# A hybrid attention and recurrent layer: the order of the first loads, and who copies x^T

## The chip, the cores and the metric

The kernel runs on one core of a Trainium2 chip. The metric is device time in microseconds (us) of one execution, the median of several. The engines of a core are TensorE (PE; its weight loads are shown apart as PEld), VectorE (DVE), ScalarE (ACT), GpSimd (POOL) and SyncE (SP, which only issues DMAs here). Each engine runs its own instructions in the order in which they stand, and waits on semaphores for the others.

## The reference

One inference step of a single decoder layer, for 1024 prompt tokens and 8 x 4 sample tokens (1056 together) with a paged cache of 1024 rows for each of the 8 sample sequences. Cut to what matters here:

```
u = rmsnorm(x, norm_mix)                       # 1056 x 1024
z = u @ w_in                                   # q, six k/v parts, gates, two RG-LRU branches
kc, vc = compress(kv rows and cached pages)    # blocks of 32 rows, stride 16, two small matmuls
o = gates * (attend(q, kc, vc), selected blocks, window of 512)
h = rglru(rx)                                  # conv of width 4, gates, a scan over time
x = x + [rmsnorm(o), rmsnorm(gelu(rg) * h)] @ w_out
x = x + square(relu(rmsnorm(x) @ w_up)) @ w_down
y = rmsnorm(x)
```

All of it is in float32. The kernel keeps that accuracy by writing each factor of a matmul as a sum of a high and a low part and taking three products.

## The kernel before

The kernel is written in stages. A list scheduler then sets each engine's order from its own estimate of times: an instruction goes where the estimate says that it can start, and `high_priority` moves a block of code ahead by a number of places. So the order on an engine is not the order of the code, and a change in one place moves rows elsewhere.

The stage that the change touches is the first, `run` up to `cmp_cached`:

- `fetch_x` loads nine tiles of x, eight of 128 tokens x 1024 (512 KB each) and one of 32 sample tokens, by SP. The pool gives eight buffers to the tag `xt`, so the ninth load waits until the first tile has been used.
- `pages_setup` loads the page table twice: to one partition for SP's registers, and as 64 single numbers to two partitions (`pt2`, issued by ACT), from which DVE casts `pf`, PE makes `ps_pg` and DVE the row numbers `idx` for POOL's gathers.
- `load_x` works in three groups of three tiles (the last has 288 columns, the others 384). ACT squares each tile with a running sum into `ss` (`xj`). Then, for each of eight blocks `kb` of 128 features, PE transposes the group's tiles into one PSUM bank, `ps_x` (even blocks from a pool of three buffers, `tp`, odd ones from a pool of two, `mm`). Three instructions empty the bank: ACT writes the scaled high part `u_hi`, DVE the rest `u_lo`, and a plain copy `xr` goes out to DRAM as x^T (`xT_dram`, POOL issues the store, one for two blocks). Of the eight `xr` copies of a group ACT makes two, DVE six.
- `w_tile` loads one 512 KB tile of w_in into the single buffer `wraw` (SP) and splits it: `wh` on ACT, `wl` on DVE. It runs at high priority, so the first of these loads stands ahead of x.
- `cmp_setup` loads the two compression weights (`cwraw`, one buffer) and splits them: the high part on ACT, the low part on POOL. `vectors` loads nine small vectors as rows of one tile (`rows`, nine DMAs of POOL), has PE turn it (`ps_vec`) and derives constants for the RG-LRU on DVE (`sp_w`, `sp_s`, `sp_acc`, `cneg`, `cpos`: a chain of tiny instructions).
- `norm_x` makes 1/rms of all tokens (`ms`, `rxi`, `rxt`, `rxy`), puts them on diagonals (`dg`, DVE), and PE spreads them over the partitions (`ps_bc`, nine products of which one is small); ACT copies the result to `R`. The first products of the layer, `ps_in` (two tiles of z, 144 matmuls), are scaled by `R` as they leave PSUM.
- `cmp_cached` gathers pages of the cache (`lpg`: half by SP, half by indirect DMAs of POOL, three buffers), copies them apart (`lpr`, POOL and DVE), and PE transposes them (`ps_ct`) for the compression matmuls `ps_c`.

DMAs of SP and ACT signal eight semaphores in turn, and a later one with the same semaphore is issued only once the earlier one has landed. After this stage come the RG-LRU, the attention (from about 400 us on) and the MLP (from about 790 us to the end).

## Time and profile before

| | |
|---|---|
| median of 3 runs | 1569.31 us (1569.22 to 1573.13) |
| profiled execution | 1570.45 us; its span 1568.7 us |
| PE busy | 1475.2 us, 94% of the span |
| PEld, DVE, ACT, POOL busy | 88%, 57%, 39%, 28% |
| mean granted TensorE clock | 0.969 |
| first matmul, first `ps_in` | 6.88 us, 42.30 us |

PE is busy almost throughout, so the time is that of PE's work and of the places at which PE has none. The largest such place is the start of the program. In the page's 40 slices of 39.2 us the first has PE at five tenths, and the DMA engines there are busy at nine tenths and move 296 GB/s, the most of all slices.

### The profile page before, as it was taken

The page shows a single profiled execution, that of the slowest core. Times are in us where ns is not written, and L with a number is a line of the kernel's source. Part 1 is how long each engine was busy: PE and PEld are TensorE (multiplying, and loading weights), DVE is VectorE, ACT ScalarE, POOL GpSimd, SP SyncE. Part 2 cuts the span into 40 slices and gives each one's busy share as a digit, 9 for nine tenths or more (in the row PEclk, how much of TensorE's full clock was granted, in tenths as well). Part 3 has the DMA queues.
Part 4 walks back from the last instruction along what each step waited for, and adds up shares of the span by engine and source line. Part 5 has one row for each costly group of instructions (what it writes and reads, how often), then busy time and mean ns, then how long its engine had stood idle before and what let it go on. Part 6 is the DMA issues. An engine that isn't in the chain of part 4 may idle for free.

```text
span 1568.7 us, 24573 instructions
## 1 busy us (share of the span) xinstructions
PE 1475.2 (94%) x9445; PEld 1381.3 (88%) x9445; DVE 890.5 (57%) x1671; ACT 615.0 (39%) x1216; POOL 440.2 (28%) x533
## 2 busy tenths in 40 slices
PE   5989999999899779999899999999999999999997
PEld 3979999999776547777898999999999999999997
DVE  6664788556687638988687343333424343342445
ACT  6253775122487528777354031220303122030322
POOL 6540143342585318767473000000000000000012
PEclk9999999999799959999999999999999999999999
DMA  9544413352013310000512020330202021020102
GB/s 296 159 149 114 125 28 106 126 174 83 28 55 90 100 55 1 1 28 28 165 47 63 13 81 28 113 102 26 69 14 81 28 68 41 19 76 14 41 13 99
DMA packets 127961, 115.53 MB, mean 74 GB/s; under 512 B 16752, under 2 KB 115760, under 8 KB 127716
## 3 DMA queue, kind: packets, MB, share of 16 engines
q1 hardware_dynamic: 122446, 102.10, 21.4%
q0 software_dynamic: 3200, 8.67, 1.8%
q10 hardware_dynamic: 2198, 3.20, 0.7%
q8 instruction: 74, 1.21, 0.3%
q14 instruction: 43, 0.35, 0.1%
HBM read 98.17 MB, written 28.32 MB: 81 GB/s over the span
## 4 chain that ended last, share of the span: by engine, by line
PE 76%; DVE 10%; ACT 6%; issue 3%; DMA 3%; POOL 2%; SPq 1%; ACTq 0%; DVEq 0%; POOLq 0%
PE ps_dn L122 8%; PE ps_dn L123 8%; PE ps_dn L124 8%; PE ps_up L122 7%; PE ps_up L123 7%; PE ps_up L124 7%; PE ps_T L1092 3%; PE ps_in L122 3%; PE ps_in L124 3%; PE ps_in L123 3%; PE ps_O L1102 2%; PE ps_out L122 2%; PE ps_out L124 2%; PE ps_out L123 2%; PE ps_O L1101 2%
## 5 line engine op out<-in xcount | busy, mean ns | idle before, releaser
L122 PE MATMUL ps_dn<-hh,wdh 128*128 128x352 f32 x768 | 248.3, 324 | 0.0
L122 PE MATMUL ps_up<-v_hi,wuh 128*128 128x352 f32 x768 | 248.1, 323 | 0.0
L123 PE MATMUL ps_up<-v_lo,wuh 128*128 128x352 f32 x768 | 246.3, 321 | 0.0
L124 PE MATMUL ps_up<-v_hi,wul 128*128 128x352 f32 x768 | 246.1, 320 | 0.0
L123 PE MATMUL ps_dn<-hl,wdh 128*128 128x352 f32 x768 | 245.9, 321 | 0.0
L124 PE MATMUL ps_dn<-hh,wdl 128*128 128x352 f32 x768 | 245.6, 321 | 0.0
L1363 DVE TENSOR_TENSOR x<-x,ps_dn 128x352 f32<-128x352 f32 x192 | 99.2, 520 | 222.2 <-PE ps_dn L124 222.2
L1428 POOL TENSOR_TENSOR facc<-facc,fsq 128x352 f32<-128x352 f32 x18 | 17.0, 942 | 700.0 <-ACT fsq L1426 699.9
L127 ACT CAST wdh<-wd 128x1024 fp32r<-128x1024 f32 x32 | 33.5, 1047 | 341.2 <-PE ps_dn L123 288.7
L123 PEld LDWEIGHTS ps_up<-v_lo,wuh 128*128 128x128 f32 x768 | 144.3, 188 | 0.0
L123 PEld LDWEIGHTS ps_dn<-hl,wdh 128*128 128x128 f32 x768 | 144.2, 188 | 0.0
L122 PEld LDWEIGHTS ps_dn<-hh,wdh 128*128 128x128 f32 x768 | 144.1, 188 | 0.0
L122 PEld LDWEIGHTS ps_up<-v_hi,wuh 128*128 128x128 f32 x768 | 144.1, 188 | 0.0
L124 PEld LDWEIGHTS ps_up<-v_hi,wul 128*128 128x128 f32 x768 | 143.9, 187 | 0.0
L124 PEld LDWEIGHTS ps_dn<-hh,wdl 128*128 128x128 f32 x768 | 143.9, 188 | 0.0
L122 PE MATMUL ps_in<-u_hi,wh 128*128 128x352 f32 x432 | 142.3, 329 | 0.0
L124 PE MATMUL ps_in<-u_hi,wl 128*128 128x352 f32 x432 | 141.0, 326 | 0.0
L123 PE MATMUL ps_in<-u_lo,wh 128*128 128x352 f32 x432 | 140.6, 326 | 0.0
L128 DVE TENSOR_TENSOR ptl<-ps_T,pth 128x512 fp32r<-128x512 f32 x132 | 87.7, 684 | 14.4 <-ACT pth L127 13.2
L127 ACT CAST pth<-ps_T 128x512 fp32r<-128x512 f32 (+1 forms) x148 | 83.1, 587 | 23.3 <-PE ps_T L1092 18.0
L122 PEld LDWEIGHTS ps_in<-u_hi,wh 128*128 128x128 f32 x432 | 82.6, 191 | 0.6 <-issue 0.3
L123 PEld LDWEIGHTS ps_in<-u_lo,wh 128*128 128x128 f32 x432 | 82.8, 192 | 0.1
(511 smaller groups left out, 3232.4 us busy)
## 6 DMA issues: line engine op xcount, KB each, us to landing
wu<-in_w_up_dram SPq DMA_DIRECT2D x32, 512.0 KB
wd<-in_w_down_dram SPq DMA_DIRECT2D x32, 512.0 KB
wraw<-in_w_in_dram SPq DMA_DIRECT2D x18, 512.0 KB
slc_dram<-in_cache_kv_dram SPq DMA_DIRECT2D x64, 128.0 KB
kvs<-slc_dram SPq DMA_DIRECT2D x32, 256.0 KB
xres<-xT_dram SPq DMA_DIRECT2D x8, 528.0 KB
x_dram<-xres SPq DMA_DIRECT2D x8, 528.0 KB
x<-x_dram SPq DMA_DIRECT2D x3, 1408.0 KB
```

Source lines behind the costliest of these rows:

```text
L122: t.matmul(out, wh, xh, start=first, stop=False)
L123: t.matmul(out, wh, xl, start=False, stop=False)
L124: t.matmul(out, wl, xh, start=False, stop=last)
L127: self.nc.scalar.copy(hi, src)
L128: (eng or self.nc.vector).tensor_tensor(lo, src, hi.bitcast(F32), ALU.subtract)
L1092: T.transpose(ps[:K, h * 128 : h * 128 + 128], src(h), self.ident)
L1101: T.matmul(O, v, ph, start=first, stop=False)
L1102: T.matmul(O, v, pl, start=False, stop=last)
L1363: V.tensor_tensor(x1[:, d, sl], x1[:, d, sl], ps[:, :CH], ALU.add)
L1428: P.tensor_tensor(acc, acc, sq, ALU.add)
```

## The change

- `fetch_x` runs at twice the priority offset of the weights, and each of the nine tiles has a buffer of its own.
- In `load_x` the squares stand behind the group's transposes in the code; ACT makes every even `xr` copy (four of eight), DVE the odd ones; `xr` has four buffers where it had five.
- `vectors` is cut in two. `vector_rows` issues the nine small loads, and only after the last store of x^T has been issued; their tile moves to the pool `ccp`. The rest of `vectors` runs after the first two tiles of z have been written.

```diff
-    def vectors(self):
-        nc, a = self.nc, self.a
-        rows = self.xrp.tile([56, 128], F32, name="rows")
+    def vector_rows(self):
+        nc, a = self.nc, self.a
+        self.rows56 = rows = self.ccp.tile([56, 128], F32, name="rows")
...
-            eng.dma_start(rows[r : r + n, :], src)
+            with self.tc.issue_after(self.stores[2, 7].ins):
+                eng.dma_start(rows[r : r + n, :], src)
             r += n
+
+    def vectors(self):
+        nc = self.nc
         ps = self.ps_c.tile([128, 512], F32, tag="c", name="ps_vec")
-        nc.tensor.transpose(ps[:, :56], rows, self.ident[:56, :56])
+        nc.tensor.transpose(ps[:, :56], self.rows56, self.ident[:56, :56])
...
         for grp in range(3):
             tiles = self.xt[grp * 3 : grp * 3 + 3]
-            for t, (xt, n) in enumerate(tiles):
-                junk = self.xtp.tile([128, D], BF16, tag="xj", name="xj", bufs=1)
-                nc.scalar.activation(junk[:n], xt[:n], AF.Square, accum_out=self.ss[:n, grp * 3 + t : grp * 3 + t + 1])
...
                 if kb % 2 == 0:
-                    xr = self.xrp.tile([128, 2, 384], F32, tag="xr", name="xr", bufs=5)
-                (nc.scalar.copy if kb % 4 == 0 else nc.vector.tensor_copy)(xr[:, kb % 2, :wdt], ps[:, :wdt])
+                    xr = self.xrp.tile([128, 2, 384], F32, tag="xr", name="xr", bufs=4)
+                (nc.vector.tensor_copy if kb % 2 else nc.scalar.copy)(xr[:, kb % 2, :wdt], ps[:, :wdt])
...
+            for t, (xt, n) in enumerate(tiles):
+                junk = self.xtp.tile([128, D], BF16, tag="xj", name="xj", bufs=1)
+                nc.scalar.activation(junk[:n], xt[:n], AF.Square, accum_out=self.ss[:n, grp * 3 + t : grp * 3 + t + 1])
...
-        for t in range(9):
-            n = 128 if t < 8 else 32
-            xt = self.xtp.tile([128, D], F32, tag="xt", name="xt", bufs=8)
-            nc.sync.dma_start(xt[:n], a["x_prompt"][0, t * 128 : t * 128 + 128] if t < 8 else xs)
-            self.xt.append((xt, n))
+        with self.tc.high_priority(offset=2 * HP):
+            for t in range(9):
+                n = 128 if t < 8 else 32
+                xt = self.xtp.tile([n, D], F32, name=f"xt{t}")
+                nc.sync.dma_start(xt, a["x_prompt"][0, t * 128 : t * 128 + 128] if t < 8 else xs)
+                self.xt.append((xt, n))
...
-                    self.vectors()
+                    self.vector_rows()
...
                 zs = [self.z_tile(512 + i * 128, self.zp, "z", 2) for i in range(2)]
+                self.vectors()
                 self.cmp_cached()
```

What the scheduler makes of it stands below, place by place. Line numbers of the changed kernel are up to five higher than those of before.

**The start, on ACT.** Before, behind its three DMA issues (`wraw` is the weight tile, `xj` the squares, `xr` the copy of x^T):

```order
L127 ACT_TABLE_LOAD
L127 CAST wh<-wraw 128x1024
L249 ACTIVATE xj,ss<-xt 128x1024 x3
L261 ACTIVATE u_hi<-ps_x,g_mix 128x384 x5
L249 ACTIVATE xj,ss<-xt 128x1024
L265 COPY xr<-ps_x 128x384
```

In the changed kernel, at the same place:

```order
L271 ACT_TABLE_LOAD
L271 ACTIVATE xj,ss<-xt_113 128x1024
L271 ACTIVATE xj,ss<-xt_115 128x1024
L271 ACTIVATE xj,ss<-xt_117 128x1024
L262 ACTIVATE u_hi<-ps_x,g_mix 128x384 x3
L271 ACTIVATE xj,ss<-xt_119 128x1024
L262 ACTIVATE u_hi<-ps_x,g_mix 128x384 x2
L266 COPY xr<-ps_x 128x384
```

The first three squares stay ahead of the first `u_hi`, though the code has them behind; the weight's cast `wh` has moved from the front to behind the eleventh `u_hi`.

**Before the first ps_in, on PE.** Before (the last transposes of x, the transposes of two gathered page tiles, and the first products):

```order
L257 MATMUL ps_x<-ident,xt 128x32
L593 MATMUL ps_ct<-ident,lpr_678 128x128 x4
L257 MATMUL ps_x<-ident,xt 128x128 x2
L257 MATMUL ps_x<-ident,xt 128x32
L593 MATMUL ps_ct<-ident,lpr_714 128x128 x4
L122 MATMUL ps_in<-u_hi,wh 128x352
```

In the changed kernel:

```order
L258 MATMUL ps_x<-ident,xt_129 128x32
L1173 MATMUL ps_bc<-dg,ones 128x128 x4
L598 MATMUL ps_ct<-ident,lpr_678 128x128 x4
L258 MATMUL ps_x<-ident,xt_125 128x128
L258 MATMUL ps_x<-ident,xt_127 128x128
L258 MATMUL ps_x<-ident,xt_129 128x32
L1173 MATMUL ps_bc<-dg,ones 128x128 x2
L598 MATMUL ps_ct<-ident,lpr_714 128x128 x4
L122 MATMUL ps_in<-u_hi,wh 128x352
```

Six of the products that spread 1/rms (`ps_bc`) have moved ahead of the first `ps_in`; before, all of them stood behind it.

**The end of the stores, on POOL.** Before (`cwvl` is the low part of the second compression weight, `lpr` a copy of a gathered page tile, `xT_dram` a store of x^T):

```order
L128 TENSOR_TENSOR cwvl<-cwraw,cwvh 128x1024
L586 COPY lpr_786<-lpg 128x256
L267 DMA xT_dram<-xr 128x2x288
L586 COPY lpr_899<-lpg 128x256
L586 COPY lpr_786<-lpg 128x256
L551 DMA lpg<-in_cache_kv_dram,idx_147 128x256 x2
```

In the changed kernel:

```order
L591 COPY lpr_786<-lpg 128x256
L268 DMA xT_dram<-xr 128x2x288
L200 DMA rows<-in_norm_mlp_dram 8x128
L200 DMA rows<-in_conv_w_dram 16x128
L200 DMA rows<-in_conv_b_dram 4x128
L200 DMA rows<-in_b_ra_dram 4x128
L200 DMA rows<-in_b_ri_dram 4x128
L200 DMA rows<-in_lam_dram 4x128
L200 DMA rows<-in_g_attn_dram 4x128
L200 DMA rows<-in_g_rnn_dram 4x128
L200 DMA rows<-in_norm_final_dram 8x128
L591 COPY lpr_899<-lpg 128x256
```

The nine small loads, which stood among POOL's first instructions, now stand behind the last store of x^T and ahead of copies and gathers of pages; `cwvl` has moved up, ahead of the third store from the end.

## Rows read from the trace of the kernel before

**Rows 1.** Stretches of the span: length, busy time of each engine, granted clock, DMA.

```profile
0.00:12.98 12.98, 4.46 (x18) 3.26 (x19) 2.28 (x11) 5.78 (x8) 7.60 (x18) 1.00 0.88 306
12.98:31.20 18.22, 10.88 (x44) 7.67 (x42) 15.98 (x31) 18.09 (x37) 13.78 (x15) 1.00 1.10 319
31.20:42.30 11.10, 6.92 (x26) 4.41 (x27) 10.86 (x42) 4.21 (x11) 7.06 (x11) 1.00 0.87 237
42.30:72.70 30.40, 29.07 (x182) 28.52 (x181) 17.14 (x45) 6.26 (x12) 19.25 (x25) 1.00 0.52 156
72.70:131.40 58.70, 53.45 (x419) 48.58 (x418) 36.49 (x81) 31.98 (x78) 19.77 (x39) 0.96 0.45 130
...
390.00:640.00 250.00, 215.62 (x1486) 161.17 (x1486) 173.44 (x357) 154.45 (x390) 139.96 (x195) 0.87 0.18 51
```

**Rows 2.** What PE waited for in 0 to 60 us: total, times, longest.

```profile
PE ps_x L257 <- DVE xr L265: 6.4, 5, 1.9
...
PE ps_pg L525 <- DVE pf L523: 1.6, 1, 1.6
```

**Rows 3.** ACT's first instructions in time: start, duration, what [idle before it].

```profile
2.12 1.28 ACT L127 ACT_TABLE_LOAD   x1 [2.12 <-issue]
4.99 1.04 ACT L127 CAST wh<-wraw 128x1024 fp32r<-128x1024 f32 x1 [1.59 <-DMA wraw<-in_w_in_dram]
6.83 1.06 ACT L249 ACTIVATE xj<-xt 128x1024 bf16<-128x1024 f32 x1 [0.80 <-DMA xt<-in_x_prompt_dram]
...
10.07 1.06 ACT L249 ACTIVATE xj<-xt 128x1024 bf16<-128x1024 f32 x1 [0.58 <-DMA xt<-in_x_prompt_dram]
...
12.98 1.52 ACT L261 ACTIVATE u_hi<-ps_x,g_mix 128x384 fp32r<-128x384 f32 x3 [1.76 <-PE ps_x L257]
```

**Rows 4.** DVE in order of time, around its first u_lo.

```profile
11.68 0.17 DVE L523 CAST pf<-pt 2x32 f32<-2x32 int32 x1 [3.73 <-DMA pt<-in_page_table_dram]
...
13.60 1.14 DVE L262 SCALAR_TENSOR_TENSOR u_lo<-ps_x,g_mix,u_hi 128x384 fp32r<-128x384 f32 x2 [0.61 <-ACT u_hi L261]
```

**Rows 5.** DVE's groups in 12.98 to 42.30 us: count | busy, mean ns | idle before.

```profile
L265 DVE COPY xr<-ps_x 128x384 f32<-128x384 f32 (+1 forms) x16 | 8.1, 519 | 0.0
...
L128 DVE TENSOR_TENSOR wl<-wraw,wh 128x1024 fp32r<-128x1024 f32 x1 | 1.2, 1224 | 0.7 <-ACT wh L127 0.7
...
L229 DVE SCALAR_TENSOR_TENSOR sp_acc<-sp_acc,sp_s 128x4 f32<-128x4 f32 x4 | 0.6, 156 | 0.0
```

**Rows 6.** ACT's groups in the same stretch.

```profile
L261 ACT ACTIVATE u_hi<-ps_x,g_mix 128x384 fp32r<-128x384 f32 (+1 forms) x24 | 12.8, 587 | 7.9 <-PE ps_x L257 7.8
...
L265 ACT COPY xr<-ps_x 128x384 f32<-128x384 f32 (+1 forms) x6 | 2.8, 474 | 0.0
```

**Rows 7.** DVE and POOL in order of time, at POOL's two weight splits.

```profile
28.55 2.35 DVE L586 COPY lpr<-lpg 128x256 f32<-128x256 f32 x1
...
32.95 0.28 DVE L586 COPY lpr<-lpg 128x256 f32<-128x256 f32 x1
...
43.28 0.59 DVE L1167 TENSOR_SCALAR dg<-ident,rxy 128x128 f32<-128x128 f32 x2
...
28.37 2.37 POOL L128 TENSOR_TENSOR cwkl<-cwraw,cwkh 128x1024 fp32r<-128x1024 f32 x1
...
45.88 2.41 POOL L128 TENSOR_TENSOR cwvl<-cwraw,cwvh 128x1024 fp32r<-128x1024 f32 x1
```

**Rows 8.** POOL in order of time: one small load, and a wait.

```profile
4.14 0.56 POOL L199 DMA_DIRECT2D rows<-in_norm_mlp_dram  x1
...
65.11 1.08 POOL L586 COPY lpr<-lpg 128x256 f32<-128x256 f32 x3 [6.41 <-PE ps_ct L593]
```

**Rows 9.** PE in order of time, around the first ps_in.

```profile
41.56 1.09 PE L593 MATMUL ps_ct<-ident,lpr 128*128 128x128 f32 x4 [1.56 <-POOL lpr L586]
42.30 0.64 PE L122 MATMUL ps_in<-u_hi,wh 128*128 128x352 f32 x1
...
54.30 0.68 PE L1168 MATMUL ps_bc<-dg,ones 128*128 128x128 f32 x4 [1.33 <-DVE dg L1167]
```

## The prediction

> **What bounds the kernel now.** I read the busy shares first: PE works 94% of the span, so a change pays only where PE has nothing to do or waits. Next the stretches [rows 1]. Up to the first `ps_in` at 42.30 us, PE is busy 4.46 + 10.88 + 6.92 = 22.3 us, with transposes alone; in the 30.4 us behind it, 29.07. The change works on the first 42.3 us, and each microsecond by which `ps_in` starts earlier shifts what follows, as long as nothing later holds PE up.
>
> What sets those 42.3 us? In 12.98 to 31.20 ACT is busy 18.09 of 18.22 us; in 31.20 to 42.30 DVE is busy 10.86 of 11.10 [rows 1]. PE's longest wait behind the first load is for DVE's `xr` copies, 6.4 us in five waits [rows 2], because a PSUM bank is free only after `u_hi`, `u_lo` and `xr`. ACT in turn waited 7.8 us for PE [rows 6], late in the stage. So there are two phases: until x has landed the loads set the pace, then ACT, and DVE at the end. The last step is a wait of 1.56 us for POOL's copy of a page tile [rows 9].
>
> **x ahead of the weights.** The weight tile landed at 4.97 us and the first x tile at 6.83, the third at 10.05 (ACT was waiting for each) [rows 3]. That is 1.6 to 1.8 us a tile of 512 KB. Without a weight tile ahead of it the third x tile should land some 1.6 us earlier, at about 8.4. ACT's table load now stands behind the first tile's arrival and takes 1.28 us, which is hidden: the tile comes at about 5.1, the load ends at 6.4, two squares of 1.06 end at 8.5, the third at 9.6. ACT's first `u_hi` moves from 12.98 to about 9.7. DVE cannot follow that far. Its cast of the page list stands ahead of its first `u_lo`, and the list landed at 11.68 after 3.73 us of waiting [rows 4]. The list's load has not moved, so the first `u_lo` goes from 13.60 to 11.85: **-1.75 us** (0 if the list lands 1.75 later, -3.7 if it no longer matters). PE's own stop of 1.6 us at `ps_pg` [rows 2] has the same cause and stays, with fifteen transposes done ahead of it. The ninth buffer frees SP from a wait before its first page load; SP's other page loads follow earlier by as much, and no one waits for them here.
>
> By the Trainium skill (DMA: Bandwidth & Descriptors, Issuing engines are not separate DMA queues), transfers of all issuing engines share the same 16 DMA engines and interleave. By that the page list, on ACT's queue, gains nothing from a new order on SP's; the trace agrees so far as it shows the list landing at 11.68 us, amid DMA engines 88% busy.
>
> **Copies from DVE to ACT.** Before the first `ps_in` DVE makes 11 copies, where it made 16 at 8.1/16 = 0.51 us [rows 5]: -2.5. ACT makes 11 where it made 5, at 2.8/6 = 0.47 [rows 6]: +2.8. ACT was busy 18.09 + 4.21 = 22.3 us between 12.98 and 42.30 [rows 1]. The order puts ahead of `ps_in` also the second weight's cast and the second compression weight's (1.04 each by the cast in rows 3) and a copy of `R` (0.6, the size of a `u_hi` [rows 6]): 22.3 + 2.8 + 2.1 + 0.6 = 27.8. Begun at 9.7 that ends at 37.5. ACT has 4.8 us to spare against 42.3, so its copies cost nothing by themselves; without that cover they would cost 2.8.
>
> **DVE's own sum.** Besides -2.5 for copies: the tiny chain behind `vectors`, 14 or so instructions of 156 ns that overlap by half [rows 5], leaves: -1.2 (-2.2 by full durations). The second `wl` comes in, +1.2 [rows 5]; three pairs of `dg` at 0.5 to 0.59 [rows 7], +1.5; the rest of the rms chain, +0.5; one more `lpr` copy, +0.3. Net **-0.2 us** (-1.2 to +0.6): DVE does other work in the place of what it loses, and that work is what it had to do later.
>
> DVE idled 29.32 - 15.98 - 10.86 = 2.5 us in 12.98 to 42.30 [rows 1], mostly for ACT. ACT now starts 3.3 us earlier, DVE 1.75; half of the idle time should go: **-1.2** (0 to -2.5).
>
> Against this stands POOL's second weight split. Beside the first one, 2.37 us on POOL, a page copy on DVE took 2.35 us where a free one took 0.28 [rows 7]: DVE stood still for 2.07. The second split ran at 45.88, after the first `ps_in`. The new order brings it before, where DVE has `dg` tiles and page copies to make: **+2.1** (0 if DVE happens to be at PSUM work then).
>
> The Trainium skill says it as a rule (Advanced Engine Details and Errata, VectorE Performance Modes): VectorE's second SBUF port is shared with GpSimd, and instructions that need it block each other. By the rule each split costs DVE up to its own length; by the copy's row it is 2.07, and the trace agrees.
>
> **Up to the first ps_in.** -1.75 - 0.2 - 1.2 + 2.1 = -1.05 us for the last transposes. The wait of 1.56 for POOL's copy [rows 9] goes too, since that copy now stands earlier among POOL's stores: -1.5 (0 to -1.56). Two `ps_bc` come in between: +0.3. First `ps_in` at 42.30 - 2.25 = **40.05 us** (36 to 43).
>
> **Behind it.** PE waited 1.33 us at 54.30 for a `dg` [rows 9]; with six `ps_bc` done ahead this goes: **-1.3** (0 to -1.33). Those six, 0.68/4 = 0.17 each [rows 9], no longer take PE's time among the products: **-1.0**. The tiny chain now runs among the compression's copies, where DVE is busy 36.49 of 58.70 us [rows 1]: **+0.6** (0 to +2.2, its whole length).
>
> POOL issues the nine small loads at about 0.52 us, 0.56 for the first [rows 8], that is 4.7 us, in front of page copies and gathers. Before, POOL idled 6.41 us until 65.11, waiting for PE's transposes [rows 8]. That idle time covers it: **0** (up to +4.7 without the cover). `ps_vec`, which needs these rows, stands 160 matmuls behind the first `ps_in`, so their landing is hidden.
>
> Squares behind the transposes: nothing by itself, the order keeps the first three ahead and ACT is not the bound. Four `xr` buffers for five: a store must have read its buffer four pairs later, over 3 us; nothing.
>
> **Later stages.** The scheduler also reorders pieces of the RG-LRU and the attention. PE idles 250 - 215.62 = 34.4 us in 390 to 640, at a mean granted clock of 0.87 [rows 1], so there is room both ways; I take 0 and +-3 us, a tenth of it.
>
> **Sum.** -2.25 - 1.3 - 1.0 + 0.6 = -3.95, say -4.0 us. Against the profiled execution's own 1570.45 us (span 1568.7, 1.75 around it) that gives 1566.45. That execution lies 1.14 above the median of the three runs, 1569.31; on the median's scale the forecast is **1565.3 us**. About 0.3%, 4.7 us, is what a measurement of this kernel can tell from no change: 1564.6 and 1574.0.
>
> **Rivals.**
> A, the start does not move: the page list lands later than before because x crowds it, or DVE stands still at both splits. Then -0.3 at the start, -1.3 behind it, +0.6: 1568.3 us. For it speaks that the list already sets DVE's start; against it, that fifteen transposes and three `u_hi` are ready by then.
> B, the second split meets DVE at PSUM work and DVE's idle time goes entirely: -1.75 - 0.2 - 2.5 - 1.2 = -5.65 at the start, then -1.3 - 1.0 and no loss in the compression: 1569.31 - 7.95 = 1561.4 us.
> C, slower: POOL becomes the one that PE waits for. Its nine issues reach the page copies after PE wants them, so 4.7 us go through to PE; the gap lets the granted clock fall once more, as it did somewhere in 72.70 to 131.40, where the mean is 0.96: 4% of 58.7 us is 2.3. On A's start that is 1568.3 + 7.0 = 1575.3 us. It decides once POOL's idle time before 65.11 is used up: POOL is busy 19.25 of 30.40 us there [rows 1], and with 4.7 more still has 6.4 free, which speaks against it.
>
> **Chances.** Forecast 0.45 (1561.5 to 1569 with its later stages), A 0.23, B 0.17, C 0.13, 0.02 for worse in the later stages. Faster by over 0.3%: half of the first and B, 0.40. Slower: C and the rest, 0.15. Between: 0.45. The range leaves out the lower end of B and most of C: 1559.5 to 1572.5.
>
> **What would show it.** In the new profile: ACT's first `u_hi` at 9 to 10 us and DVE's first `u_lo` at 11.5 to 12; a DVE row of over 2 us beside `cwvl` before the first `ps_in`; that `ps_in` at 39 to 41; no wait for `dg` behind it; POOL's nine `rows` inside a stretch in which PE does not wait for `lpr`. The forecast is wrong if `ps_in` starts at 42 or later, if PE waits for page tiles between 60 and 110 us, or if the attention loses or wins more than 3 us.

## The result: slower, by 1.3%

| | before | changed |
|---|---|---|
| median | 1570.53 us (1569.22 to 1573.13) | **1591.71 us** (1589.60 to 1592.73) |
| ratio, 95% interval | | **1.0131** [1.0111, 1.0152] |
| profiled execution, its span | 1570.45, 1568.7 us | 1592.30, 1590.4 us |
| mean granted clock | 0.969 | 0.962 |

The forecast was 1565.3 us in a range of 1559.5 to 1572.5. The time came out 19 us above the range's upper end, on the side that held a chance of 0.15. None of the mechanisms named for the start brought it; the reordering of the later stages was named, and taken at 0 with 3 us either way. In these two profiles the span grew by 21.7 us. Span times (1 - mean clock) is 48.6 us before and 60.4 after, so some 11.8 of these 21.7 us go with a lower clock; in a second profile of the changed kernel (span 1585.3 us, clock 0.965) it is 6.9 of 16.6. Of the four executions of the kernel h2 below, one took 1841.9 us at a mean granted clock of 0.83, and medians and ratios leave it out.

The table cuts the span at instructions that both kernels have: the first `ps_in`, the first `ps_st` (the RG-LRU), the first `ps_gt`, the first `ps_cs` (the attention), the second `ps_ot` (half of it) and the first `ps_up` (the MLP). Lengths in us; "again" is a second profile of the changed kernel.

| stretch | before | changed | again | h1 | h2 |
|---|---|---|---|---|---|
| to the first `ps_in` | 42.3 | 46.6 | 46.8 | 47.8 | 42.1 |
| to the RG-LRU | 106.2 | 108.2 | 107.5 | 105.5 | 107.2 |
| RG-LRU | 120.6 | 126.1 | 125.6 | 120.6 | 125.4 |
| to the attention | 136.5 | 138.9 | 138.7 | 137.8 | 138.9 |
| attention, first half | 167.9 | 167.4 | 168.5 | 169.7 | 169.4 |
| second half, `ps_out` | 229.8 | 237.9 | 232.8 | 228.9 | 232.5 |
| MLP | 765.3 | 765.3 | 765.4 | 765.5 | 767.1 |

So the start, where a gain of 2.25 us was expected, lost 4.3, and the stages behind it, taken at 0, lost some 17 in this execution and 12 in the second.

Part of such differences is there in one order too. Most kernels of the experiments below have before's order in the late stages, and three profiles have the changed kernel's (changed, again, h2). How far the lengths lie apart within each (us; the number of profiles in brackets):

| stretch | before's order | the changed kernel's order (3) |
|---|---|---|
| RG-LRU | 120.6 to 120.8 (11) | 125.4 to 126.1 |
| to the attention | 135.8 to 138.7 (11) | 138.7 to 139.0 |
| attention, first half | 167.9 to 171.5 (9) | 167.4 to 169.4 |
| second half, `ps_out` | 228.1 to 233.6 (9) | 232.5 to 237.9 |

So the 5 us of the RG-LRU are clear. The 2 us up to the attention lie at the upper end of what before's order takes, and the 3 to 8 of the second half lie only in part above it. The stretch behind the first `ps_in` took 106.2 us before and 101.6 in a kernel that differs from before in the attention alone (f7), so the 1 to 2 us more in that stretch are not shown to be an effect.

The stretches of the changed kernel, in the columns of [rows 1]; the first two answer to its first two, the last two to rows of before that follow:

```profile
0.00:12.98 12.98, 6.24 (x23) 4.17 (x23) 3.42 (x15) 8.19 (x15) 3.89 (x10) 1.00 0.86 316
12.98:31.20 18.22, 9.56 (x36) 6.37 (x36) 11.49 (x24) 15.59 (x32) 12.80 (x15) 1.00 1.03 278
...
154.80:280.90 126.10, 117.86 (x708) 116.14 (x708) 95.91 (x130) 80.80 (x118) 36.96 (x45) 0.96 0.25 71
...
587.20:824.90 237.70, 219.82 (x1331) 185.53 (x1332) 187.51 (x332) 148.38 (x300) 146.23 (x147) 0.93 0.12 39
```

Before, the RG-LRU and the attention's two halves:

```profile
148.50:269.20 120.70, 116.21 (x719) 114.21 (x719) 96.80 (x132) 81.07 (x119) 39.77 (x47) 1.00 0.27 77
405.70:573.60 167.90, 138.03 (x1025) 98.19 (x1026) 114.56 (x260) 104.81 (x286) 92.80 (x149) 0.84 0.27 76
573.60:803.20 229.60, 213.87 (x1332) 180.60 (x1333) 184.82 (x332) 147.58 (x300) 147.32 (x147) 0.95 0.13 40
```

Two things are to be seen. In 12.98 to 31.20 ACT and DVE, which had 18.09 and 15.98 us of work there before [rows 1], have 15.59 and 11.49. Of ACT's difference 2.4 us is work that it had done before 12.98 us, of DVE's 1.1; so it is DVE above all that waits. And in the RG-LRU PE works as long as before but for 1.65 us, and the stretch is 5.4 us longer: 8.2 us idle for 4.5, and the clock at 0.96 for 1.00.

### The start of the changed kernel

ACT in order of time, as in [rows 3]:

```profile
9.42 1.51 ACT L262 ACTIVATE u_hi<-ps_x,g_mix 128x384 fp32r<-128x384 f32 x3
...
20.57 1.04 ACT L127 CAST wh<-wraw 128x1024 fp32r<-128x1024 f32 x1 [0.17 <-DMA wraw<-in_w_in_dram]
...
26.06 1.04 ACT L127 CAST cwkh<-cwraw 128x1024 fp32r<-128x1024 f32 x1 [2.46 <-DMA cwraw<-in_w_ck_dram]
```

DVE, as in [rows 4, 7]:

```profile
9.95 0.17 DVE L528 CAST pf<-pt 2x32 f32<-2x32 int32 x1 [2.84 <-DMA pt<-in_page_table_dram]
10.04 0.60 DVE L263 SCALAR_TENSOR_TENSOR u_lo<-ps_x,g_mix,u_hi 128x384 fp32r<-128x384 f32 x1
...
28.56 1.01 DVE L288 TENSOR_SCALAR ms<-ss 128x9 f32<-128x9 f32 x1 [3.51 <-ACT xj L271]
...
41.64 2.73 DVE L591 COPY lpr<-lpg 128x256 f32<-128x256 f32 x1
```

PE, as in [rows 9]:

```profile
27.54 3.20 PE L258 MATMUL ps_x<-ident,xt 128*128 128x128 f32 x12 [2.46 <-ACT xr L266]
...
41.22 1.22 PE L1173 MATMUL ps_bc<-dg,ones 128*128 128x128 f32 x4 [0.18 <-DVE dg L1172]
...
44.88 1.20 PE L1173 MATMUL ps_bc<-dg,ones 128*128 128x128 f32 x4 [0.92 <-DVE dg L1172]
46.58 0.64 PE L122 MATMUL ps_in<-u_hi,wh 128*128 128x352 f32 x1
```

SP's issue of the first compression weight, before and then changed (start, time on SP):

```profile
12.99 4.26 SPq L466 DMA_DIRECT2D cwraw<-in_w_ck_dram  x4
```

```profile
11.82 8.73 SPq L471 DMA_DIRECT2D cwraw<-in_w_ck_dram  x4
```

Read from the bottom: the loads of `cwraw` stand behind x's first eight tiles in both kernels (what the change put behind x is `wraw`, for whose cast ACT waits only 0.17 us). SP begins the four loads of `cwraw` 1.2 us earlier than before, but is through with them at 20.55 us, where it was at 17.25. In the kernels below with the weights first they take SP 4.0 to 4.4 us (5.9 in f6), in those with x first 4.6 to 8.7; why is not shown. The DMA engines are full either way, with a share of 1.10 before and 1.03 after in 12.98 to 31.20 us.

ACT comes to the cast of this tile at 23.6 us and stands still for 2.46 us. Behind that cast, in ACT's order, are a copy of x^T that frees a PSUM bank, for which PE waits 2.46 us, and the last square, for which DVE's `ms` waits 3.51 us; behind `ms` stand DVE's next `u_lo` and `xr`. Before, ACT reached the same cast at 26.27 us and waited for nothing. ACT's start at 9.42 us was about as forecast, and of its lead of 3.6 us only 0.2 is left at this cast.

That takes the gain away, but not more. The rest of the loss comes later. There are 24 blocks of transposes, and so 24 `u_lo`. The next rows cut DVE's time at the start of its first, its 20th and its last `u_lo`, before and then changed (DVE's busy time is the third after the length):

```profile
13.60:36.23 22.63, 12.80 (x50) 8.64 (x49) 21.00 (x47) 18.80 (x39) 16.20 (x19) 1.00 1.03 299
36.23:40.57 4.34, 3.64 (x14) 2.25 (x13) 4.10 (x20) 2.03 (x6) 2.42 (x4) 1.00 0.88 234
```

```profile
10.04:35.67 25.63, 13.78 (x51) 8.76 (x50) 18.90 (x46) 21.07 (x43) 16.64 (x20) 1.00 1.05 295
35.67:45.09 9.42, 5.93 (x22) 4.38 (x23) 9.01 (x22) 4.98 (x12) 8.93 (x10) 1.00 1.00 272
```

The changed kernel leads by 3.56 us at the first `u_lo` and still by 0.56 at the 20th; DVE had 2.1 us less to do up to there, but stood idle for 6.7 us instead of 1.6. Over the last four blocks it falls 4.5 us behind (9.42 us for 4.34; it is 9.42 in all four profiles of this start). There DVE is busy nearly throughout in both kernels, and has 9.01 us of work for 4.10: the new order puts the second `wl`, the 1/rms chain and the `dg` tiles between the last `u_lo`, and a page copy that takes 2.73 us.

### The RG-LRU of the changed kernel

Four stretches of it (PE's clock is the third column from the right):

```profile
200.00:217.00 17.00, 15.38 (x95) 14.94 (x93) 14.02 (x18) 12.06 (x16) 6.50 (x8) 1.00 0.22 64
217.00:230.00 13.00, 11.42 (x60) 11.14 (x61) 11.11 (x18) 9.49 (x15) 0.54 (x2) 0.87 0.15 42
230.00:245.00 15.00, 13.77 (x87) 13.48 (x85) 13.23 (x13) 11.42 (x15) 8.66 (x7) 1.00 0.00 0
245.00:258.00 13.00, 9.51 (x45) 9.22 (x46) 12.00 (x17) 8.88 (x14) 5.29 (x4) 0.74 0.15 42
```

PE's waits at the head of the second and of the fourth of them:

```profile
217.59 0.43 PE L122 MATMUL ps_g<-xh,w_rah 128*128 128x360 f32 x1 [2.21 <-ACT xh L127]
219.98 0.29 PE L416 MATMUL ps_l<-ident,lt 128*36 128x128 f32 x1 [0.99 <-POOL lt L414]
```

```profile
245.59 0.43 PE L122 MATMUL ps_g<-xh,w_rah 128*128 128x360 f32 x1 [1.82 <-ACT xh L127]
249.56 0.40 PE L416 MATMUL ps_l<-ident,lt 128*36 128x128 f32 x1 [2.90 <-POOL lt L414]
```

All of PE's waits in this stage, in total, times, longest; changed, and then before:

```profile
PE ps_l L416 <- POOL lt L414: 4.2, 3, 2.9
PE ps_g L122 <- ACT xh L127: 4.0, 2, 2.2
```

```profile
PE ps_g L123 <- DVE xl L128: 2.0, 2, 1.1
PE ps_g L122 <- ACT xh L127: 1.3, 1, 1.3
PE ps_g L122 <- ACT t L391: 1.1, 1, 1.1
```

In the new order `ps_l`, the transpose of a scan's last values, stands ahead of products that are ready, and `ps_g` ahead of other products of the layer. PE waits in pairs, 2.2 and 1.0 us, 1.8 and 2.9 us, and at each pair the clock falls to its lower level of 1.2 GHz: for 3.4 us from the first pair on, and for 6.8 from 247.5 us on, within the second (13 us at a mean of 0.87 and of 0.74). In the second profile the clock falls at the same two places, for 6.8 and then 3.4 us. Before, with no wait over 1.3 us, it stays at 2.4 GHz throughout. Of the wait of 2.90 us for `lt`, 1.99 are a copy of 128 x 1 numbers on POOL, which takes 0.19 to 0.41 us elsewhere in this stage and runs here beside DVE's split of a weight.

### The profile page after: what moved, and what is told of

It reads as the page before. It is cut to its first block, busy times and chain, and to the rows that moved or that the text cites. A ratio compares the mean times of both kernels' runs of the same rounds, so it can differ in the third digit from the quotient of the medians.

```text
span 1590.4 us, 24573 instructions
## 1 busy us (share of the span) xinstructions
PE 1489.8 (94%) x9445; PEld 1394.0 (88%) x9445; DVE 892.2 (56%) x1665; ACT 620.2 (39%) x1222; POOL 437.4 (28%) x533
## 4 chain that ended last, share of the span: by engine, by line
PE 51%; DVE 2%; ACT 1%; POOL 1%; issue 0%; DMA 0%; DVEq 0%; ACTq 0%; POOLq 0%
PE ps_dn L122 8%; PE ps_dn L123 8%; PE ps_dn L124 8%; PE ps_up L122 7%; PE ps_up L123 7%; PE ps_up L124 7%; PE ps_out L122 1%; PE ps_T L1097 1%; PE ps_out L124 1%; PE ps_out L123 1%; PE ps_O L1106 1%; PE ps_O L1107 1%; PE ps_f L1437 0%; DVE x L1342 0%; PE ps_S L1065 0%
## 5 line engine op out<-in xcount | busy, mean ns | idle before, releaser
L127 ACT CAST pth<-ps_T 128x512 fp32r<-128x512 f32 (+1 forms) x148 | 83.1, 588 | 31.6 <-PE ps_T L1097 24.1
```

The lines of the kernel that those rows point to most:

```text
L127: self.nc.scalar.copy(hi, src)
```

## Experiments

In each, the ratio is to the kernel before on the same chip, with its 95% interval. In all but the changed kernel's second profile and the `memset` kernel the order was held by extra edges between neighbours on each engine, from a list (no run has such edges around an order that the kernel had anyway, so what they cost by themselves is not measured): in h1, h2 and the single parts that of the late work (all that the code has from the RG-LRU's setup on), in the others that of everything.

### Is it the start, or the order behind it?

The changed kernel with before's late order (h1), and the kernel before with the changed kernel's late order (h2). Both have the same edit, with different lists:

```diff
     k.run()
+    late_order(tc, mark[0])
```

> The changed kernel, with everything from the RG-LRU's setup on (from about 115 us of the span) put on each engine in exactly the order of the kernel before. Theory (order): the changed kernel's 21.7 us of span are 4.3 us up to the first ps_in and some 17 us behind 131 us, and the second part comes from the new order alone, so this kernel gives 1591.7 - 17 = 1574.5 us (1572 to 1577), with PE's waits for lt gone and the first ps_in still at about 46.6 us. Rival (state): the late loss comes from what the new start leaves behind (later loads, constants that come late, other addresses), whatever the order: then 1588 to 1592 us.

Measured: 1577.82 us, 1.0046 [1.0025, 1.0066]; just above the theory's 1577.

> The kernel before, unchanged in its code, with everything from the RG-LRU's setup on in the order of the changed kernel. Theory (order): first ps_in at 42.3 us as before, then the late loss of some 17 us: 1569.3 + 17 = 1586.5 us (1583 to 1589), and the same waits of PE for lt and xh as in the changed kernel. Rival (state): the old start keeps the late stages as they were: 1569 to 1571 us.

Measured: 1585.96 us (the median of three), 1.0109 [1.0063, 1.0155]; as the theory had it. The stages are in the table above, and two of them here, the RG-LRU and the attention's second half. h1:

```profile
153.30:274.00 120.70, 116.16 (x719) 114.14 (x719) 96.86 (x132) 81.45 (x119) 39.75 (x47) 1.00 0.29 81
...
581.50:810.20 228.70, 210.77 (x1331) 178.72 (x1332) 185.69 (x332) 147.32 (x300) 146.68 (x147) 0.97 0.13 41
```

h2:

```profile
149.30:274.70 125.40, 117.42 (x707) 115.61 (x707) 96.16 (x129) 79.82 (x117) 36.42 (x45) 0.96 0.25 71
583.00:815.40 232.40, 211.88 (x1331) 178.88 (x1332) 186.94 (x332) 148.10 (x300) 146.34 (x147) 0.97 0.13 40
```

With the old order the RG-LRU takes 120.7 us at a clock of 1.00 behind the new start; with the new order it takes 125.4 at 0.96 behind the old start. So these 5 us belong to the order and not to what the start leaves behind; of the second half's 8, some 3 come with the order in h2, within what one order's profiles differ by. By the ratios the new start costs some 7 us and the new late order some 17, with 7 either way; together 24, where the change as a whole costs 20 to 21. The theory of a state that the start leaves behind, with the order of no account, falls with h2.

### Which part of the change costs the start?

One part each in the kernel before, all with before's late order:

```diff
# x_first_lb (and xr in four buffers instead of five)
-        for t in range(9):
+        with self.tc.high_priority(offset=2 * HP):
+            for t in range(9):
...
-            xt = self.xtp.tile([128, D], F32, tag="xt", name="xt", bufs=8)
...
+                xt = self.xtp.tile([n, D], F32, name=f"xt{t}")
# copies_lb
-                (nc.scalar.copy if kb % 4 == 0 else nc.vector.tensor_copy)(xr[:, kb % 2, :wdt], ps[:, :wdt])
+                (nc.vector.tensor_copy if kb % 2 else nc.scalar.copy)(xr[:, kb % 2, :wdt], ps[:, :wdt])
# vectors_lb
...
-                    self.vectors()
+                    self.vector_rows()
...
+                self.vectors()
                 self.cmp_cached()
```

> The kernel before with x ahead of the weights and nine buffers alone (the x^T buffers go from five to four to make room), late work in the order of before. Theory (weights late): the casts of weights stand in order on ACT and DVE, and wait for tiles that now land behind x; that is the start's loss, so the first ps_in comes at 45 to 47 us and the time is 1569.3 + 3 to 4.5 = 1572 to 1574 us. Rival (copies): the loss at the start comes from ACT's added copies; then x alone brings the first ps_in to 40 to 42 us and the time to 1567 to 1569 us.

Measured: 1581.10 us, 1.0061 [1.0040, 1.0083]; first `ps_in` at 49.04 us.

> The kernel before with half of the x^T copies on ACT alone, late work in the order of before. Theory (weights late): the copies are hidden or help a little, first ps_in at 41 to 42.5 us, 1568 to 1570 us. Rival (copies): ACT becomes the bound of the start, first ps_in at 45 to 47 us, 1572 to 1574 us.

Measured: 1574.36 us, 1.0021 [1.0003, 1.0039]; first `ps_in` at 41.17 us.

> The kernel before with the small vectors loaded and worked on later, alone, late work in the order of before. Theory (weights late, casts): the chain of tiny instructions leaves DVE's full stretch, first ps_in 0.5 to 1.5 us earlier, at 41 to 42 us, and the nine DMA issues of POOL (4.7 us) are hidden in its idle time: 1567 to 1570 us. Rival (POOL): page copies come late behind the nine issues, PE waits for lpr between 55 and 110 us, 1572 to 1575 us.

Measured: 1575.71 us, 1.0031 [1.0011, 1.0052]; first `ps_in` at 40.01 us.

x ahead of the weights delays the first `ps_in` by 6.7 us, more than the 3 to 5 that were expected, and the time is above the theory's 1574; the rival, that the copies cost it, is out. The copies bring 1.1 us and the vectors 2.3, and neither brings time: both kernels are a little slower than before, where 1568 to 1570 and 1567 to 1570 us were expected. With `vectors_lb` PE does not wait for `lpr`, so POOL's issues are not the reason; what it is stays open. The squares had no run of their own. The parts do not add up: 0.61, 0.21 and 0.31% for h1's 0.46. Of the 6.7 us with x ahead, 1.9 are matmuls of PE that came ahead of `ps_in` (busy 24.1 us for 22.25): this order, too, puts the twelve rows of `ps_bc` there. The rest is waiting. ACT waits for the same tile as in the changed kernel, longer:

```profile
27.91 1.04 ACT L127 CAST cwkh<-cwraw 128x1024 fp32r<-128x1024 f32 x1 [4.28 <-DMA cwraw<-in_w_ck_dram]
```

### Does the start recover when the casts are out of the way?

h1 with the compression weights' casts (`cwkh`, `cwvh` on ACT, `cwkl`, `cwvl` on POOL) behind the transposes of x (f1), and with the page list as ACT's first load besides (f2). ACT's order:

```diff
-L127 CAST cwkh<-cwraw 128x1024
 L266 COPY xr<-ps_x 128x384
...
-L127 CAST cwvh<-cwraw 128x1024
 L266 COPY xr<-ps_x 128x288
...
 L262 ACTIVATE u_hi<-ps_x,g_mix 128x288
+L127 CAST cwkh<-cwraw 128x1024
```

> The kernel of the first experiment (new start, late work in the old order), with one thing moved in the start: the casts of both compression weights on ACT, their low parts on POOL and the second one's loads on SP stand behind the x transposes instead of among them. Theory (weights late): the casts hold ACT, and behind it DVE, PE and POOL, until weights land that now stand behind x; without them first ps_in comes 2.5 to 4.5 us earlier, at 42 to 45 us, and the time is 1577.8 - 3.5 = 1574 us (1572 to 1576). Rival (page list): DVE's start is set by the page list, which lands at 10 to 15 us; then the casts change at most 1 us.

Measured: 1583.72 us, 1.0088 [1.0064, 1.0111]; first `ps_in` at 44.6 us.

> As the kernel above, with ACT's load of the page list issued as its first instead of its third. Theory (weights late): the list is not what counts, first ps_in within 1 us of the kernel above. Rival (page list): the list lands by 8 us instead of 10 to 15, DVE's first u_lo starts behind the first u_hi at about 10 us, and first ps_in comes 2 to 5 us earlier than in the kernel above.

Measured: 1583.30 us, 1.0089 [1.0069, 1.0109]; first `ps_in` at 43.2 us.

The start moved as the theory has it, from 46.6 to 47.8 us in three profiles to 44.6, and by 1.4 more with the list ahead, between what the two expectations had. f1's edit takes two things out, ACT's wait for `cwraw` and the slow page copy beside `cwvl`, and does not tell them apart. And it does not bring the start back to before's 42.3. The last four blocks still take twice their time there, though DVE is not full:

```profile
34.64:43.51 8.87, 6.30 (x24) 4.78 (x25) 6.79 (x22) 3.50 (x10) 7.05 (x10) 1.00 0.97 269
```

From the 20th `u_lo` to the last it is 8.9 to 10.1 us in all seven profiles of kernels that have the twelve rows of `ps_bc` ahead of `ps_in`, 4.9 to 6.0 in the four that have four of them, and 4.2 to 4.4 in the five that have none. The second `wl` and the `dg` tiles come with them; no run tells which of these it is.

The time rose, where 1572 to 1576 us was expected. The stretch behind the first `ps_in` grew from h1's 105.5 to 115.1 us, and one wait has most of that. In f1, PE's wait, then DVE and SP in order of time:

```profile
PE ps_bc L1173 <- DVE dg L1172: 9.8, 1, 9.8
```

```profile
60.85 0.29 DVE L591 COPY lpr<-lpg 128x256 f32<-128x256 f32 x1 [13.63 <-DMA lpg<-in_cache_kv_dram]
```

```profile
51.07 2.66 SPq L471 DMA_DIRECT2D cwraw<-in_w_cv_dram  x4
57.44 8.60 SPq L552 DMA_DIRECT2D lpg<-in_cache_kv_dram  x4
```

With `cwkl` late, SP's second set of `cwraw` loads waits for its buffer, and the page loads wait behind it in SP's queue; DVE waits 13.63 us for a page tile with `dg` behind that copy. So a moved instruction takes with it whatever its buffer holds up, as in the prediction whatever waits for its tile.

### Is it the transposes of the scan's last values that hold up the RG-LRU?

The changed kernel again, and the same with the first three `ps_l` 80 matmuls later on PE (and their copies `last` later on DVE). PE, at the first:

```diff
 L124 MATMUL ps_in<-u_hi,wl 128x352
-L416 MATMUL ps_l<-ident,lt 36x128
 L123 MATMUL ps_g<-xl,w_rah 128x360
...
 L122 MATMUL ps_in<-u_hi,wh 128x352
+L416 MATMUL ps_l<-ident,lt 36x128
 L123 MATMUL ps_in<-u_lo,wh 128x352
```

> The changed kernel once more, beside the three that follow. Both theories: 1588 to 1593 us. What it tells is whether the granted clock falls at the same places of the attention (32 us at half clock between the first of the attention's second half and the MLP in the first trace, 13 in the run that had the same order behind the old start): theory (order) expects the falls of the RG-LRU again, 10 us at half clock there, since they follow waits; those of the attention may move.

Measured: 1588.33 us, 1.0129 [1.0106, 1.0151]. The falls of the clock in the RG-LRU came again (125.6 us at a mean of 0.96), as the theory had it; the attention's second half took 232.8 us at 0.97, where it was 237.9 at 0.93.

> The changed kernel in its own order, with the first three ps_l transposes of the RG-LRU 80 matmuls later on PE, and their copies to last correspondingly later on DVE; nothing needs them before the stage's end. Theory (order): PE's waits for POOL's lt (4.2 us) and the fall of the clock behind them (up to 4 us) go: 1591.7 - 4 to - 8 = 1584 to 1588 us. Rival: PE then waits as long for the next product, ps_g, whose xh and xl come from the same chain of DVE and POOL: 1590 to 1592 us.

Measured: 1588.55 us, 1.0136 [1.0103, 1.0168]. The RG-LRU and its waits:

```profile
151.00:275.30 124.30, 116.56 (x707) 113.72 (x707) 96.38 (x129) 78.86 (x116) 36.25 (x45) 0.99 0.26 74
```

```profile
PE ps_g L122 <- ACT xh L127: 5.8, 3, 2.9
PE ps_g L123 <- DVE xl L128: 1.3, 2, 1.1
PE ps_l L416 <- POOL lt L414: 0.7, 1, 0.7
```

The wait for `lt` went from 4.2 to 0.7 us, and most of it came back at `xh`: the products of the gates stand too early on PE as well. The stage won 1.3 to 1.8 us, mostly clock (0.99), and the time won nothing (1588.55 us lies between the two expectations, and beside it the changed kernel took 1588.33). These three rows alone are not at fault; the rest of the order was not tested row by row.

### What is an order worth?

Two starts put in order by hand, with before's late order. f5 is before with the new copies, and with the second and third weight tiles' casts, the compression weights' casts, the small vectors' chain and the loads that belong to them behind the transposes of x; f4 is the same with x ahead. On DVE in f5:

```diff
 L262 SCALAR_TENSOR_TENSOR u_lo<-ps_x,g_mix,u_hi 128x384
-L128 TENSOR_TENSOR wl<-wraw,wh 128x1024
...
 L1167 TENSOR_SCALAR dg<-ident,rxy 128x128 x2
+L1167 TENSOR_SCALAR dg<-ident,rxy 128x128 x2
+L128 TENSOR_TENSOR wl<-wraw,wh 128x1024
```

> The kernel before with half of the x^T copies on ACT, weights still loaded ahead of x, late work in the order of before, and the start's order changed by hand: the second weight's casts, the compression weights' splits, the chain of tiny constants on DVE and the loads that wait for them stand behind the last transposes of x. Theory (casts): ACT and DVE, which are full between 13 and 42 us, lose some 2.3 and 4.5 us of work and of standing still beside POOL, so the first ps_in moves from 41.2 us to 38 to 39.5, and the time to 1566 to 1568 us. Rival (loads): x lands no earlier, DMA engines are nine tenths busy to 31 us, and the start is theirs: first ps_in at 40.5 to 41.5 us, 1569 to 1571 us.

Measured: 1570.88 us, 0.9995 [0.9976, 1.0014]; first `ps_in` at 37.62 us.

> The kernel above with x ahead of the weights into nine buffers, the first weight's casts placed late in the x stage on ACT and DVE, where the tile has landed. It tells what x ahead is worth when no cast waits among the transposes. Theory (casts): x ahead by itself gains 1 to 3 us at the start, first ps_in at 36 to 38 us. Rival (idle time): the first weight's casts (1.04 us on ACT, 1.22 on DVE) move from a time when both engines wait for x into one when both are full, and the page list lands later, so x ahead gives nothing: first ps_in at 39 to 41 us, as late as without it or later.

Measured: 1580.47 us, 1.0058 [1.0038, 1.0078]; first `ps_in` at 39.01 us.

With the weights first, f5 starts its products 4.7 us earlier than before, as expected, is 4.1 us ahead when the attention begins, and has 0.5 of that left at its middle: the first half took 171.5 us, where before, in the same order, took 167.9. But that order took 167.9 to 171.5 us in nine profiles, so a loss of this size in one profile is within what executions differ by. The time is that of before (0.9995), where 1566 to 1568 us was expected.

With x ahead the start is 1.4 us longer than f5's, as the rival had it, and the stretch behind it 5.9, and the kernel 0.6% slower. It is not shown that x ahead costs this: f4's list differs from f5's in other places too. SP issues the page loads from the seventh on only at 42.26 us, where f5 issues twelve in a row from 20.23 on; between 38 and 75 us DVE waits 8.0 us for page tiles where it waits 5.2 in f5, with `z` behind them, and PE waits 3.7 us for `z` where it waits 0.2.

The third is before with one instruction of the setup on another engine, which makes no difference by itself:

```diff
-        nc.vector.memset(self.ones, 1.0)
+        nc.gpsimd.memset(self.ones, 1.0)
```

> The kernel before with one instruction on another engine: the memset of the ones tile (0.17 us) on POOL instead of DVE. Nothing is computed, loaded or waited for in another way, but the scheduler's order of the late stages comes out in 954 of 8513 places on PE and 258 of 1455 on DVE otherwise than before. Theory (order): the time moves by more than the memset can: by 2 us or more, either way, with the first ps_in at 42 to 43 us. Rival: an edit without work does not move the time, 1568 to 1570 us.

Measured: 1568.40 us, 0.9986 [0.9966, 1.0005]. The scheduler answered this edit with another order in hundreds of places from about 42 us on. The time alone decides nothing: its interval reaches from no change, as the rival had it, to some 5 us less. Its stages stood at -3.3 us (the attention's first half, 164.6), +2.4 (up to the attention, 138.9) and +2.6 (up to the RG-LRU, 108.8), and only the first lies clearly outside what before's order takes. So its order of the attention alone went into before (f7), and into f5 (f6). ACT's first difference there in f7 (`qtc` and `Ps` belong to the attention's queries and scores):

```diff
 L982 CAST qtr<-zqr 64x2x128 x6
+L982 CAST qtc<-zq 64x2x128 x2
 L1040 ACTIVATE Ps,dens<-ps_S,nms 128x128 x4
-L982 CAST qtc<-zq 64x2x128 x2
```

> The kernel before in its own start and RG-LRU order, with that attention order alone. Theory (order): first half of the attention 163 to 167 us, the rest as before, 1565 to 1568 us, ratio 0.997 to 0.999. Rival (clock gives back): 1569 to 1572 us, ratio within 0.001 of 1.

Measured: **1564.05 us**, 0.9963 [0.9947, 0.9978].

> The start changed by hand (first ps_in at 37.6 us there), the RG-LRU in the order of the kernel before, and the attention in the order of the kernel with the moved memset, whose first half took 164.6 us where the order of before takes 167.4 to 171.5. Theory (order, stages add up): the start's gain of 4.7 us and the attention's of some 3 to 5 both stay: span 1561 to 1565, time 1563 to 1567 us, ratio 0.995 to 0.998. Rival (clock gives back): the attention's granted clock falls for longer when its waits are shorter or it begins earlier, and takes back what was won, as it took 4 us in the kernel with the start by hand: 1569 to 1572 us.

Measured: **1564.49 us**, 0.9957 [0.9937, 0.9977]. Both beat both kernels; f7 is a little better than expected, and f6, as expected by its time, is no better than f7. f7's first half of the attention:

```profile
402.70:567.00 164.30, 137.75 (x1024) 99.38 (x1025) 115.64 (x259) 105.67 (x286) 92.47 (x149) 0.84 0.27 78
```

f7 waits 164.30 - 137.75 = 26.6 us there, where before waited 29.9, at the same clock of 0.84: a gain of the order. The three profiles with this order (164.3, 164.6, 165.3) lie below all nine with before's. (The profiled execution of f7 is faster by more than that: it has a clock of 1.00 behind the first `ps_in`, in the same order for which the profile of before has 0.95.)

An earlier start did not show in the time. The copies, the vectors and f5 start `ps_in` 1.1, 2.3 and 4.7 us earlier than before, and their times stand at 1.0021, 1.0031 and 0.9995; f6 starts 3.6 us earlier than f7 and stands at 0.9957 beside 0.9963. Why is open.

## Why the prediction was wrong, step by step

**Right.** ACT's first `u_hi` at 9.42 us (forecast 9.7). DVE's work between its first `u_lo` and the first `ps_in`: 29.24 us for 26.83, so +2.41, of which the copy beside the split is 2.45 (forecast -0.2 and +2.1). The second split of POOL did meet a page copy on DVE, 2.73 us where a free one takes 0.28: 2.45 us (forecast 2.1). By the Trainium skill (Advanced Engine Details and Errata, VectorE Performance Modes), GpSimd instructions and VectorE instructions that need its second SBUF port block each other; this trace agrees (2.73 us for 0.28). POOL's nine loads stayed hidden, so rival C is out: POOL then idles until PE wants pages,

```profile
49.97 0.67 POOL L200 DMA_DIRECT2D rows<-in_norm_mlp_dram  x1
...
73.23 0.40 POOL L591 COPY lpr<-lpg 128x256 f32<-128x256 f32 x1 [12.43 <-PE ps_ct L598]
```

and those 12.43 us are more than the 6.4 that were counted on. The wait for `lpr` ahead of `ps_in` is gone. So is the wait of 1.33 us for `dg` behind it, of which 0.92 came ahead of `ps_in` instead.

**x ahead of the weights, the first `u_lo`.** Forecast 11.85, came at 10.04, since the page list landed 1.7 us earlier than in the profile of before. That was luck: in seven profiles with x ahead and the list in its place DVE cast it between 7.85 and 15.22 us, in eight with the weights first between 11.34 and 12.29. In h1 it came at 15.2 us and PE waited 5.5 us for it. "The list's load has not moved" was right of its issue and says little of its landing amid x. The forecast did not hang on it either: in four profiles of this start the first `u_lo` came at 10.04, 12.48, 13.12 and 15.31 us, and `ps_in` at 46.58, 48.47, 46.83 and 47.81.

**"Up to the first ps_in", -2.25: the step that failed at the start.** It came out at +4.3, and the term that failed is DVE's idle time: forecast -1.2 ("half of the idle time should go"), measured +5.4. From its first `u_lo` to `ps_in` DVE idled 7.3 us, where it was 1.87 before, and 3.51 of that is the wait for the last square behind `cwkh` on ACT. Each cast that the order moved was priced at its own duration, and ACT's sum ended with 4.8 us to spare. But an engine in order that waits for a tile holds what stands behind it, and ACT, being earlier, now came to `cwkh` before its tile was there: 2.46 us on ACT, 3.51 on DVE behind it, 2.46 and more on PE. The question who stands behind a tile on each engine was asked for the page list and not for the weights. And DVE's work was right as a sum but not in its place: 2.1 us left where DVE then idled, and 4.9 came in over the last four blocks, where it was full. Rival A, the start that doesn't move, was the nearest for the start, and had the wrong tile.

The sum also took it that what the start gains stays to the end. The copies, the vectors, f5 and f6 beside f7 don't show it.

**The six `ps_bc`, +0.3 and -1.0.** Each of the six products is two rows in the trace, twelve together, so that the row of before at 0.17 was half of a product. They run ahead of `ps_in` at 1.22/4 = 0.305 us a row, 3.6 us in all, against some 2 us that they no longer take behind it: at most +1.7 where -0.7 stood, and less where they fill time in which PE would have waited for DVE.

**"Later stages", 0 +-3: the term that was mis-sized most.** It came out at +12 to +17 in the two profiles, and h2, with before's start, stands at 1.0109, some 17 us. In the profiles it is 5 in the RG-LRU, 2 up to the attention, 3 to 8 in the attention's second half and 1 to 2 in the stretch behind `ps_in`; of these only the RG-LRU's 5 are clear of what one order's profiles differ by. The argument took a tenth of the attention's idle time as room both ways and did not look at the RG-LRU, where PE had only 4.5 us of idle time and a clock of 1.00, so that there was little to win and more to lose. The order of both kernels was there to be read: `ps_l` and `ps_g` had moved ahead of ready products. And the clock was counted only in rival C, though 11.8 of 21.7 us go with it in one profile and 6.9 of 16.6 in the other.

**What stays open.** The attention's second half took 237.9 us in one profile of the changed kernel and 232.8 in the other, by the same order; the first at a clock of 0.93, the second at 0.97. What decides it is not known. Nor is which of the rows that the new order puts between the last four blocks holds them up in f1, or why an earlier `ps_in` does not show in the time.

## What to carry to other kernels

An engine that starts earlier gains only up to its first instruction whose tile is not there yet, and all that stands behind that instruction waits with it: price a cast by the landing of its tile, and list who stands behind it on each engine. Ask also where in a stage work is added: the sum can be right, and the time lost where the engine is full. Where a scheduler sets the order, an edit at the start is also an edit of every later stage: hold the later order fixed to measure the edit, and take the order itself as a thing to be chosen on the chip, where one picked out of a null edit gave 0.4%; no part of this change gained any time. A dense stage with the clock at its upper level and little idle time has little room to win and can lose twice, by the wait and by the clock behind it.

## What was not expected of the hardware

- In the RG-LRU of the changed kernel two pairs of waits of 1.0 to 2.9 us went with 3.4 and 6.8 us at the lower clock (6.8 and 3.4 in the second profile); the waits of up to 2.9 us in the kernel with the later `ps_l` came with a mean of 0.99.
- The stretch from the first `ps_in` to the RG-LRU took 106.2 us at a mean clock of 0.95 in one profile and 101.6 at 1.00 in another, in the same order (before, f7).
- A page list of 64 numbers, issued in the same place, was used between 7.85 and 15.22 us with x ahead of the weights, and between 11.34 and 12.29 with the weights first.
- POOL is slowed by DVE too: a copy of 128 x 1 numbers took 1.99 us on POOL from 247.40 us on, beside DVE's split of a weight at 247.26, and 0.19 to 0.41 us elsewhere in that stage. It took 1.99 us there in both profiles of the changed kernel, and 1.10 in h2.
